# Dilated attention's second stage: places of GpSimd's transfers, a fourth maxima tile, gate and high part in two steps, later residual loads

## The chip, the cores and the metric

The program runs on one NeuronCore of a Trainium2 chip. The metric is device microseconds of one execution. An engine has its own instruction stream and works through it in order: TensorE (PE, its weight loads PEld), VectorE (DVE), ScalarE (ACT), GpSimd (POOL) and SyncE (SP). Semaphores tie them together. A transfer is issued from a queue of one of these engines and lands later; an instruction that waits holds up all that stands behind it on its engine.

## The reference

A trunk of two layers on a sequence of 1024 tokens with 1024 channels, all in float32: layer 0 mixes by a gated short convolution, layer 1 by dilated attention. Only the second part of layer 1 is touched. For 16 head slots and three dilation groups (windows and dilations 128/1, 512/4, 2048/16) it computes

```python
for g, (window, dilation) in enumerate(DILATED_GROUPS):
    q = rms_norm(qkv[:, :, g, 0], q_gain[g])
    k = rms_norm(qkv[:, :, g, 1], k_gain[g])
    o, l = dilated_group_attention(q, k, qkv[:, :, g, 2], bias_g, window, dilation)
...
alpha = jax.nn.softmax(jnp.stack(lses, axis=0), axis=0)
o = jnp.sum(alpha[..., None] * jnp.stack(outs, axis=0).astype(jnp.float32), axis=0)
y = o.reshape(B, S, ATTN_WIDTH).astype(h.dtype) * jax.nn.silu(z)
return y @ w_out        # and the layer adds x
```

where a group's attention is the softmax over a causal band of 128-query blocks with a table of position biases, and l is the log of its denominator.

## The kernel before

The convolution layer and the projection of the attention layer come first and leave q and k (qkd), v (vd), silu(z) (zd) and the residual stream (x1d) in device memory. The second stage takes them from there. Its work is cut into 24 units: eight pairs of heads (hp 0 to 7), each with groups g = 0, 1, 2. A unit has 4, 4 and 2 steps for the three groups, so a pair has ten and the stage has 80 steps; step 0 of pair hp is step 10 hp of the stage. Steps below are counted over the whole stage unless "of its pair" is said.

The order on each engine is written out by hand: a loop over k goes through the parts of the steps that are due, in the order of lags (0, 1, LC = 4, 3, 5 to 16, LB = 2), then the exps, then the dense tiles (`extra`), then what is started ahead (`begins`). A part with lag n of step j is issued in turn k = j + n. Within a turn, each engine gets its instructions in that order.

A step has four parts. A: scores on PE (L904, L918, L923) and on DVE, for each block and head, an addition of the bias that also takes the running minimum of the negated scores into the unit's small tile `nl` (L936). E: the exps on ACT (L942), which also leave the row sums in `nl`. B, two turns later: transposes on PE (L949) into a bank of `pt`, copied to `pts` by DVE (L860) or ACT (L862). C, four turns later: the product with V on PE (L963, L970) and, when a half of the output is complete, its copy into `o` by DVE (L982, L985).

The three groups of a pair are merged by their denominators. The groups order tokens differently, so the maxima and sums of groups 0 and 1 go through device memory on POOL's queue: `store` writes `nl` to `nld` (L994 for g = 0, L997 twice for g = 1), and for g = 2 loads them back in its own order into `ml` (L992, twice). `weights` takes the overall maximum on DVE (L1006 to L1009) and one exp on ACT (L1010). `shares` makes the three factors `fo` on DVE (L1019 to L1024), `store_shares` writes them to `fd` (L1028, twice), and `spread` reads each back over 64 partitions, into `fb` for w = 2 and 1 and into `sqacc` for w = 0 (L1033, six transfers). `scale` multiplies a group's output by its factor (L1036, three times on DVE), `add` sums two of them on POOL (L1039, twice), `gate` multiplies by silu(z) in `sz` (L1042, DVE), `high` rounds the result to the first of two parts `y2` (L1046, ACT), and `low` takes the remainder (L1049, DVE). Pair 6 has an earlier schedule than pairs 0 to 5, and pair 7 ends the stage by other means (`wide`, `spread_last`, `last`).

The tile `nl` has three buffers that the units take in turn; `begin` takes a new one in the first part A of a unit. `fo`, `ml`, `f`, `mx` and `sqacc` have one buffer each.

The output projection rides along: `some` computes one of 16 tiles of the output for two pairs at a time, six matmuls a step (L1133 to L1135), from step k0 = (first step of pair 2r + 2) + LD on; in the next turn DVE adds the sum to the tile's accumulator (`add_sums`, L1169), which `residual` filled from x1d (L1150) on SP's queue. The third block starts at step 74 and runs past the loop's 80 steps. `fetch`, `split` (L1144) and `split_low` (L1147) bring in the weights of the projection and cut them in two parts. SP's queue also carries the loads of q and k (`loads`), V (`load_v`), sz (`load_z`) and the bias tables (`prefetch`).

Of the kernel before, what the change touches and what calls it, by code (L numbers as in the profile page):

```python
# [10 lines left out]
F32 = mybir.dt.float32  # L11
F32R = mybir.dt.float32r
I32 = mybir.dt.int32
AF = mybir.ActivationFunctionType
# [21 lines left out]
def trunk(ctx: ExitStack, tc: tile.TileContext, a, out):  # L36
# [778 lines left out]
    with tc.tile_pool(name="sp", bufs=1, space=PSUM) as sp, tc.tile_pool(name="ptp", bufs=2, space=PSUM) as ptp, \  # L815
# [48 lines left out]
        def attention(hp, g):  # L864
# [18 lines left out]
            def begin():  # L883
                u["nl"] = sm.tile([P, 8, 4], F32, name="nl", tag="nl", bufs=3)

# [114 lines left out]
            def weights():  # L1000
# [8 lines left out]
                nc.vector.tensor_tensor(f[:, :, 2], mx[:, :, 0], nm, op=OP.subtract)  # L1009
                nc.scalar.activation(f, f, AF.Exp)  # L1010
                u["f"] = f, mx
# [23 lines left out]
            def scale(w):  # L1035
                nc.vector.tensor_tensor(O[hp, w], O[hp, w], u["fb", w], op=OP.mult)  # L1036
# [66 lines left out]
            end = steps[-1]  # L1103
            end.setdefault(0 if g == 2 else 1, []).append(store)
            if g == 2:
# [6 lines left out]
                else:  # L1112

                    e = -1 if hp == HP - 2 else 1 - hp % 2
                    w = 2 if e < 0 else 3
                    todo = [(w, weights), (w + 1, shares), (w + 1, store_shares), (w + 1, lambda: spread(2)),
                            (w + 1, lambda: spread(1)), (w + 1, lambda: spread(0)), (e + 9, lambda: scale(2)),
                            (e + 10, lambda: scale(1)), (e + 10, lambda: add(2)), (e + 11, lambda: scale(0)),
                            (e + 11, lambda: add(0)), (e + 13, gate), (e + 13, high), (e + 14, low)]
                for lag, f in todo:  # L1120
# [3 lines left out]
        LB, LC = 2, 4  # L1124
        LD = 14
        W, ending = {}, {}
# [30 lines left out]

        sums = []

# [28 lines left out]
        for i, (dt, hf) in enumerate(tiles):  # L1188
            when(3 + 2 * i, residual, dt, hf)
        for r in range(3):  # L1190
# [11 lines left out]
        for kt in range(KT):  # L1202
            k = at[kt // 2 * 2 + 2, 0][0] + 4 + kt % 2 if kt < 6 else len(steps) - 6 + kt % 2
            when(k - 5 - kt % 2, fetch, kt)
            when(k, split, kt)
            when(k + 2, split_low, kt)
# [5 lines left out]
        while k < len(steps) + LC - 1 or any(x >= k for x in extra):  # L1212
# [4 lines left out]
            for f in steps[k].get("exps", ()) if k < len(steps) else ():  # L1217
                f()
            for f in extra.get(k, ()):
                f()  # L1220
            for f in begins.get(k, ()):
                f()
            k += 1

# [93 lines left out]
```

## Time and profile before

| | |
|---|---|
| median of three runs | 1984.29 us (1981.63 to 1986.51) |
| the profiled execution | 1977.11 us |
| its span on the page | 1975.3 us |
| attention's second stage, loop | from about 1626 us on |
| transfers from 1625 to 1960 us | 66.69 MB, 199 GB/s on average |

The page divides the span into 40 slices, with a busy share in tenths for each engine and the TensorE clock that was granted:

```profile
PE   8999999999999999999999999999999998798998
...
DVE  7866765666576555788889689868998867788896
ACT  6433333333334453444343443334334338777670
POOL 0356657766665211334434344444434351332330
PEclk9999999999999999999999999999999998899999
DMA  6312232222224574413233233323233357976752
GB/s 197 116 57 92 82 107 76 95 93 78 96 65 158 181 237 166 141 67 119 95 117 118 79 114 107 122 72 128 88 106 107 106 174 252 268 222 200 211 146 86
```

A slice is 49.4 us wide; the second stage fills the last seven, from slice 33 on (counted from 0). A busy share there says how much of a slice an engine worked, not what it waited for: that is read from the waits view and the timeline, in which a row gives the start, the duration, the engine and line, output and inputs, and in brackets the idle time ahead of the instruction with the instruction or transfer that ended it.

### The profile page before, as it was taken

The numbers are of one execution on the slowest core, as the hardware profiler recorded it, in microseconds if no ns is written. First come the engines' busy times: TensorE is split into PE (matmuls) and PEld (weight loads), VectorE is DVE, ScalarE is ACT, GpSimd is POOL, SyncE is SP. The second block draws the span as 40 slices with busy tenths as digits, with TensorE's granted clock in tenths as the row PEclk, the third lists the DMA queues.
The fourth block names the chain that finished last, engine by engine and source line by source line (L and its number), as shares of the span: only waits on it lengthen the run. The fifth ranks groups of instructions, "written<-read, shape, count | busy, mean of one in ns | idle before, by whom it ended". The sixth has DMA issues, their size and how long they took to land.

```text
span 1975.3 us, 30620 instructions
## 1 busy us (share of the span) xinstructions
PE 1910.9 (97%) x10894; PEld 1553.3 (79%) x10894; DVE 1495.4 (76%) x2769; ACT 885.8 (45%) x2031; POOL 848.5 (43%) x767
## 2 busy tenths in 40 slices
PE   8999999999999999999999999999999998798998
PEld 6888888888888888878878888788888876576767
DVE  7866765666576555788889689868998867788896
ACT  6433333333334453444343443334334338777670
POOL 0356657766665211334434344444434351332330
PEclk9999999999999999999999999999999998899999
DMA  6312232222224574413233233323233357976752
GB/s 197 116 57 92 82 107 76 95 93 78 96 65 158 181 237 166 141 67 119 95 117 118 79 114 107 122 72 128 88 106 107 106 174 252 268 222 200 211 146 86
DMA packets 116777, 253.79 MB, mean 128 GB/s; under 512 B 17598, under 2 KB 22814, under 8 KB 116624
## 3 DMA queue, kind: packets, MB, share of 16 engines
q1 hardware_dynamic: 93280, 176.89, 28.0%
q0 software_dynamic: 23344, 74.95, 11.3%
q8 instruction: 85, 1.39, 0.3%
q14 instruction: 68, 0.56, 0.1%
HBM read 192.53 MB, written 67.64 MB: 132 GB/s over the span
## 4 chain that ended last, share of the span: by engine, by line
PE 77%; DVE 12%; issue 5%; DMA 3%; ACT 3%; POOL 1%; SPq 0%; DVEq 0%; POOLq 0%; ACTq 0%
PE pp L301 18%; PE pp L304 18%; PE pp L303 17%; PE pp L552 3%; PE pp L551 3%; PE pp L553 3%; DVE ws L165 2%; PE pt L949 2%; PE po L970 2%; DVE blkc L716 1%; PE pp L374 1%; PE pp L375 1%; PE pp L376 1%; DMA nld<-nl 1%; ACT xs L942 1%
## 5 line engine op out<-in xcount | busy, mean ns | idle before, releaser
L165 DVE TENSOR_TENSOR ws<-wr,ws 128x512 fp32r<-128x512 f32 x284 | 279.0, 984 | 120.9 <-ACT ws L164 119.5
L164 ACT ACTIVATE ws<-wr 128x512 fp32r<-128x512 f32 x284 | 178.3, 630 | 357.9 <-PE pp L304 232.6
L164 ACT ACTIVATE ws<-sr 128x512 fp32r<-128x512 f32 x272 | 169.9, 629 | 293.2 <-PE pp L304 235.7
L276 POOL TENSOR_TENSOR sr<-wr 128x512 f32<-128x512 f32 x136 | 186.6, 1372 | 259.9 <-DMA wr<-in_wqk 59.2
L165 DVE TENSOR_TENSOR ws<-sr,ws 128x512 fp32r<-128x512 f32 x272 | 226.6, 840 | 70.9 <-ACT ws L164 68.7
L313 DVE TENSOR_TENSOR f<-pp,f 128x512 f32<-128x512 f32 x204 | 139.6, 684 | 91.0 <-PE pp L304 84.3
L942 ACT ACTIVATE xs<-xs,nl 128x256 f32<-128x256 f32 (+2 forms) x384 | 160.5, 425 | 5.4 <-DVE nl L936 5.3
L309 ACT ACTIVATE f<-pp 128x512 f32<-128x512 f32 x228 | 132.5, 581 | 27.8 <-POOL blkc L682 12.5
L671 ACT ACTIVATE f<-f 128x512 f32<-128x512 f32 x96 | 60.7, 632 | 139.2 <-DVE f L313 101.8
L276 POOL TENSOR_TENSOR sr<-wr,sr 128x512 f32<-128x512 f32 x68 | 88.5, 1301 | 70.7 <-issue 47.8
L936 DVE CUSTOM_DVE_ANT_0 xs<-ps,bt 128x256 f32<-128x256 f32 (+2 forms) x384 | 102.3, 325 | 21.8 <-PE ps L923 8.8
L301 PE MATMUL pp<-blkg,ws 128*128 128x512 f32 x272 | 107.2, 394 | 3.5 <-ACT f L309 3.5
L301 PE MATMUL pp<-blkf,ws 128*128 128x512 f32 x272 | 108.5, 399 | 0.7 <-ACT f L309 0.7
L301 PE MATMUL pp<-blka,ws 128*128 128x512 f32 x272 | 107.1, 394 | 0.7 <-ACT f L309 0.7
L301 PE MATMUL pp<-blkb,ws 128*128 128x512 f32 x272 | 107.4, 395 | 0.0
L301 PE MATMUL pp<-blkd,ws 128*128 128x512 f32 x272 | 106.9, 393 | 0.0
L304 PE MATMUL pp<-blkf,ws 128*128 128x512 f32 x272 | 106.3, 391 | 0.0
L304 PE MATMUL pp<-blkb,ws 128*128 128x512 f32 x272 | 106.0, 390 | 0.0
L304 PE MATMUL pp<-blka,ws 128*128 128x512 f32 x272 | 106.0, 390 | 0.0
L304 PE MATMUL pp<-blkd,ws 128*128 128x512 f32 x272 | 106.0, 390 | 0.0
L303 PE MATMUL pp<-blkb,ws 128*128 128x512 f32 x272 | 105.9, 389 | 0.0
L303 PE MATMUL pp<-blka,ws 128*128 128x512 f32 x272 | 105.9, 389 | 0.0
(341 smaller groups left out, 5270.4 us busy)
## 6 DMA issues: line engine op xcount, KB each, us to landing
wr<-in_conv_w_in SPq DMA_DIRECT2D x128, 256.0 KB, 3.1
wr<-in_wqk SPq DMA_DIRECT2D x96, 256.0 KB, 3.0
qkd<-blkc POOLq DMA_DIRECT2D x48, 512.0 KB, 3.4
qk<-qkd SPq DMA_DIRECT2D x48, 512.0 KB, 5.2
wr<-in_conv_w_out SPq DMA_DIRECT2D x64, 256.0 KB, 3.2
f<-in_x SPq DMA_DIRECT2D x48, 256.0 KB, 4.3
wr<-in_wv SPq DMA_DIRECT2D x48, 256.0 KB, 3.1
vd<-f POOLq DMA_DIRECT2D x48, 256.0 KB, 2.6
```

Source lines behind the costliest of these rows:

```text
L164: nc.scalar.activation(t[:, 0], src, AF.Copy)
L165: nc.vector.tensor_tensor(t[:, 1], src, t[:, 0].bitcast(F32), op=OP.subtract)
L276: nc.gpsimd.tensor_tensor(t, x, y, op=op)
L301: nc.tensor.matmul(ps, w[:, 0, ws], b[:, k, 0], start=new and k == 0, stop=False, skip_group_check=not new)
L303: nc.tensor.matmul(ps, w[:, 0, ws], b[:, k, 1], start=False, stop=False, skip_group_check=not new)
L304: nc.tensor.matmul(ps, w[:, 1, ws], b[:, k, 0], start=False, stop=end and k == 3, skip_group_check=not new)
L309: nc.scalar.activation(t, ps, AF.Copy)
L313: nc.vector.tensor_tensor(m, ps, m, op=OP.add)
L551: nc.tensor.matmul(ps[dt], w[:, 0, ws], b[:, k, 0], start=(q == k == 0), stop=False)
L671: nc.scalar.activation(sq, t, AF.Square)
L936: nc.vector.tensor_tensor_reduce(out=x, in0=flat[s][:, cols], in1=u["bt"][s][:, bs], op0=OP.add, op1=OP.min, scale=-1.0, scalar=3e38, accu ...
L942: nc.scalar.activation(x, x, AF.Exp, bias=nm, scale=-1.0, accum_out=L)
```

## The change

Counted in the whole stage, for pair hp with first step 10 hp:

- `nl` has four buffers instead of three.
- The stores of groups 0 and 1 keep their lag of 1. The load of `ml` moves from lag 0 of the pair's last step to lag 2 for pairs 0 and 1 and lag 1 for pairs 2 to 5; pairs 6 and 7 keep 0.
- `weights` moves from step 12 to 13 for pairs 0 and 1 and stays at 12 for pairs 2 to 5. `shares` and `store_shares` move from 13 to 14, `spread` from 13 to 16. The three `scale` stay at 19, 20, 21 for even pairs and go from 18, 19, 20 to the same places for odd pairs, with `add` in the steps of the last two.
- `gate` goes from 23 to 22 for even pairs and stays at 22 for odd ones; `high` is at 23 and `low` at 24 for both (before: 23 and 24 for even, 22 and 23 for odd pairs). Pair 6 keeps its places (weights 11, shares 12, scales 17 to 19, gate and high 21, low 22) except for `spread`, which goes from 12 to 13.
- The exp of `weights` is put in a list, `behind`, that is emptied after the exps of the turn.
- LD is 15 instead of 14: the dense tiles are at steps 35 to 50, 55 to 70 and from 75 on instead of 34, 54 and 74; five instead of six tiles of the third block lie within the 80 steps.
- The 16 residual loads are at steps 31 to 46, one a step, instead of 3, 5, ... 33.
- The split of every odd row of the projection's weights, both its parts, comes a step later; the fetches stay.

```diff
@@ -881,7 +881,7 @@
                 u["bt"] = bt
 
             def begin():
-                u["nl"] = sm.tile([P, 8, 4], F32, name="nl", tag="nl", bufs=3)
+                u["nl"] = sm.tile([P, 8, 4], F32, name="nl", tag="nl", bufs=4)
 
             def nml(j, s):
                 return u["nl"][:, j, s:s + 1], u["nl"][:, j, 2 + s:3 + s]
@@ -1007,7 +1007,7 @@
                 nc.vector.tensor_tensor(mx[:, :, 0], mx[:, :, 0], nm, op=OP.min)
                 nc.vector.tensor_tensor(f[:, :, 0:2], mx.to_broadcast([P, 8, 2, 2]), ml[:, :, :, 0:2], op=OP.subtract)
                 nc.vector.tensor_tensor(f[:, :, 2], mx[:, :, 0], nm, op=OP.subtract)
-                nc.scalar.activation(f, f, AF.Exp)
+                behind.append(lambda: nc.scalar.activation(f, f, AF.Exp))
                 u["f"] = f, mx
 
             def shares():
@@ -1101,7 +1101,7 @@
                     st = make(js, not steps)
                     steps.append({lag: [f] for lag, f in zip((0, LB, LC, "exps"), st)})
             end = steps[-1]
-            end.setdefault(0 if g == 2 else 1, []).append(store)
+            end.setdefault(1 if g < 2 else 2 if hp < 2 else 1 if hp < HP - 2 else 0, []).append(store)
             if g == 2:
                 if hp == HP - 1:
                     steps[-2][3] = steps[-2].pop(LC)
@@ -1111,18 +1111,20 @@
                     ending.update(turn=end.pop(LB)[0], weights=weights, spread=spread_last, last=last)
                 else:
 
-                    e = -1 if hp == HP - 2 else 1 - hp % 2
-                    w = 2 if e < 0 else 3
-                    todo = [(w, weights), (w + 1, shares), (w + 1, store_shares), (w + 1, lambda: spread(2)),
-                            (w + 1, lambda: spread(1)), (w + 1, lambda: spread(0)), (e + 9, lambda: scale(2)),
-                            (e + 10, lambda: scale(1)), (e + 10, lambda: add(2)), (e + 11, lambda: scale(0)),
-                            (e + 11, lambda: add(0)), (e + 13, gate), (e + 13, high), (e + 14, low)]
+                    todo = [(2, weights), (3, shares), (3, store_shares), (4, lambda: spread(2)),
+                            (4, lambda: spread(1)), (4, lambda: spread(0)), (8, lambda: scale(2)),
+                            (9, lambda: scale(1)), (9, lambda: add(2)), (10, lambda: scale(0)),
+                            (10, lambda: add(0)), (12, gate), (12, high), (13, low)] if hp == HP - 2 else [
+                            (4 if hp < 2 else 3, weights), (5, shares), (5, store_shares), (7, lambda: spread(2)),
+                            (7, lambda: spread(1)), (7, lambda: spread(0)), (10, lambda: scale(2)),
+                            (11, lambda: scale(1)), (11, lambda: add(2)), (12, lambda: scale(0)),
+                            (12, lambda: add(0)), (13, gate), (14, high), (15, low)]
                 for lag, f in todo:
                     end.setdefault(lag, []).append(f)
             return steps, prefetch
 
         LB, LC = 2, 4
-        LD = 14
+        LD = 15
         W, ending = {}, {}
 
         def dense(ps, kts, dt, hf, first, last):
@@ -1155,7 +1157,7 @@
             t = scores() if name == "ps" else ptp.tile([P, 4, P], F32, name=name, tag=name)
             return t.rearrange("p a b -> p (a b)")
 
-        sums = []
+        sums, behind = [], []
 
         def some(kts, dt, hf, name):
 
@@ -1186,7 +1188,7 @@
             if un[1] == 2:
                 when(k - 1, load_z, un[0])
         for i, (dt, hf) in enumerate(tiles):
-            when(3 + 2 * i, residual, dt, hf)
+            when(31 + i, residual, dt, hf)
         for r in range(3):
             k0 = at[2 * r + 2, 0][0] + LD
             k = k0
@@ -1200,8 +1202,8 @@
                                                some((2 * r, 2 * r + 1), dt, hf, name))
                 k += (i % 2 if i < 13 else 0) if late else 1
         for kt in range(KT):
-            k = at[kt // 2 * 2 + 2, 0][0] + 4 + kt % 2 if kt < 6 else len(steps) - 6 + kt % 2
-            when(k - 5 - kt % 2, fetch, kt)
+            k = (at[kt // 2 * 2 + 2, 0][0] + 4 if kt < 6 else len(steps) - 6) + 2 * (kt % 2)
+            when(k - 5 - 2 * (kt % 2), fetch, kt)
             when(k, split, kt)
             when(k + 2, split_low, kt)
         when(len(steps), ending["turn"])
@@ -1216,10 +1218,14 @@
                     f()
             for f in steps[k].get("exps", ()) if k < len(steps) else ():
                 f()
+            while behind:
+                behind.pop()()
             for f in extra.get(k, ()):
                 f()
             for f in begins.get(k, ()):
                 f()
+            while behind:
+                behind.pop()()
             k += 1
```

How the instructions stand on the engines, at three places. First POOL's queue, from the load of pair 0's maxima on, before (DMA rows are transfers; `x2` is two of a kind in a row):

```order
L992 DMA ml<-nld 64x64 x2
L1028 DMA fd<-fo 64x6x8 x2
L1033 DMA fb<-fd 64x1024 x4
L1033 DMA sqacc<-fd 64x1024 x2
L994 DMA nld<-nl 128x8x4
L997 DMA nld<-nl 512x1x4 x2
L992 DMA ml<-nld 64x64 x2
L1039 TENSOR_TENSOR o<-o 128x1024 x2
```

and in the changed kernel:

```order
L992 DMA ml<-nld 64x64 x2
L994 DMA nld<-nl 128x8x4
L1028 DMA fd<-fo 64x6x8 x2
L1033 DMA fb<-fd 64x1024 x4
L1033 DMA sqacc<-fd 64x1024 x2
L997 DMA nld<-nl 512x1x4 x2
L1039 TENSOR_TENSOR o<-o 128x1024 x2
L992 DMA ml<-nld 64x64 x2
```

Pair 1's store of group 0 (L994) now stands ahead of pair 0's factors and their spread, and pair 1's load of `ml` behind pair 0's two additions.

Second, DVE in steps 42 to 44, as the difference of the two orders, where pair 2 is gated (L1042) and pair 3 weighted (L1006 to L1009, then L1019 to L1024). Step 42:

```order
 L1008 TENSOR_TENSOR f<-mx,ml 128x8x4
 L1009 TENSOR_TENSOR f<-mx,nl 128x8x2
+L1042 TENSOR_TENSOR sz<-o,sz 128x1024
 L860 COPY pts<-pt 128x384
-L1169 TENSOR_TENSOR acc<-pd,acc 128x512
+L1171 TENSOR_TENSOR acc<-pd,acc 128x512
```

The gate is now behind pair 3's weights (the addition of a dense tile only has another line number). The piece with the shares, step 43 before and 44 in the changed kernel:

```order
 L1023 RECIPROCAL mx<-mx 128x16
 L1024 TENSOR_TENSOR fo<-f,mx 128x8x6
-L1042 TENSOR_TENSOR sz<-o,sz 128x1024
```

The gate no longer stands behind the shares.

Third, ACT in steps 41 to 43 before, with the exp of pair 3's weights (L1010) and pair 2's high part (L1046):

```order
L862 ACTIVATE pts<-pt 128x256 x2
L942 ACTIVATE xs,nl<-xs,nl 128x256 x4
L1010 ACTIVATE f<-f 128x48
L862 ACTIVATE pts<-pt 128x384
L942 ACTIVATE xs,nl<-xs,nl 128x256 x4
L1046 ACTIVATE y_15555<-sz 128x1024
L862 ACTIVATE pts<-pt 128x512 x2
```

and in the changed kernel:

```order
L862 ACTIVATE pts<-pt 128x256 x2
L942 ACTIVATE xs,nl<-xs,nl 128x256 x4
L862 ACTIVATE pts<-pt 128x384
L942 ACTIVATE xs,nl<-xs,nl 128x256 x4
L1010 ACTIVATE f<-f 128x48
L1046 ACTIVATE y_15525<-sz 128x1024
L862 ACTIVATE pts<-pt 128x512 x2
```

The exp of the weights now follows the exps of its step instead of standing ahead of that step's copy; the high part stays ahead of the copies of the next step.

## The prediction

> **What bounds the kernel now.** First the head of the page and its clock row, then the windows view by head pair, since a share of the whole span hides the one stage that is edited.
>
> ```profile
> span 1975.3 us, 30620 instructions
> ...
> PEclk9999999999999999999999999999999998899999
> ```
>
> The profiled execution took 1977.11 us, 1.8 us more than its span and 7.2 us under the median 1984.29. The sum is made against 1977.1, and its difference is then taken from the median. The granted clock falls under 0.9 in only two of the 40 slices, from 1630 to 1728 us, inside the edited stage. Everything before 1626 us is the same code in both kernels.
>
> ```profile
> 1626.00:1649.00 23.00, 20.75 (x301) 15.20 (x301) 18.15 (x103) 20.77 (x80) 3.48 (x4) 1.00 0.83 270
> 1649.00:1683.00 34.00, 27.18 (x413) 21.48 (x410) 23.94 (x127) 25.02 (x111) 8.70 (x14) 0.85 0.76 238
> 1683.00:1724.00 41.00, 28.89 (x407) 21.66 (x406) 30.97 (x121) 27.88 (x113) 12.71 (x15) 0.83 0.96 263
> ```
>
> Columns: stretch, length, busy PE, PEld, DVE, ACT, POOL with counts, granted clock, DMA share, GB/s. The rows are ten steps each: pairs 0, 1 and 2. Pair 0 takes 2.3 us a step at full clock; pairs 1 and 2 take 34 and 41 us though no engine is busy for more than 31. The rest is waiting. PE's timeline gives the places; the bracket is the idle time ahead of the row and its releaser.
>
> ```profile
> 1664.73 1.94 PE L949 MATMUL pt<-ident,xs 128*128 128x128 f32 x8 [6.54 <-DVE pts L860]
> ...
> 1693.27 1.55 PE L923 MATMUL ps<-qk 64*64 64x192 f32 x14 [7.12 <-DVE nl L936]
> ...
> 1702.29 1.06 PE L949 MATMUL pt<-ident,xs 128*128 128x128 f32 x8 [1.01 <-DVE pts L860]
> ...
> 1704.51 0.88 PE L970 MATMUL po<-pts,V 128*64 128x128 f32 x12 [0.51 <-DVE o L982]
> ...
> 1708.19 2.00 PE L949 MATMUL pt<-ident,xs 128*128 128x128 f32 x8 [2.80 <-DVE pts L860]
> ...
> 1737.29 0.63 PE L949 MATMUL pt<-ident,xs 128*128 128x128 f32 x4 [3.53 <-DVE pts L860]
> ...
> 1782.45 1.20 PE L949 MATMUL pt<-ident,xs 128*128 128x128 f32 x8 [2.87 <-ACT pts L862]
> ...
> 1810.82 0.44 PE L949 MATMUL pt<-ident,xs 128*128 128x128 f32 x2 [0.61 <-DVE pts L860]
> ...
> 1816.47 0.63 PE L949 MATMUL pt<-ident,xs 128*128 128x128 f32 x4 [0.91 <-DVE pts L860]
> ...
> 1860.58 1.14 PE L949 MATMUL pt<-ident,xs 128*128 128x128 f32 x8 [2.86 <-ACT pts L862]
> ...
> 1889.68 0.44 PE L949 MATMUL pt<-ident,xs 128*128 128x128 f32 x2 [1.36 <-DVE pts L860]
> ...
> 1896.52 0.63 PE L949 MATMUL pt<-ident,xs 128*128 128x128 f32 x4 [2.10 <-DVE pts L860]
> ```
>
> After a gap PE runs at a lower clock, which the windows behind the gaps show:
>
> ```profile
> 1665.00:1686.00 21.00, 21.00 (x270) 16.34 (x268) 17.68 (x89) 18.22 (x80) 6.89 (x11) 0.86 0.82 231
> 1693.00:1705.00 12.00, 10.21 (x160) 7.99 (x162) 11.77 (x42) 6.70 (x27) 5.81 (x4) 0.79 0.91 302
> 1708.00:1734.00 26.00, 24.32 (x378) 18.47 (x378) 21.99 (x103) 25.40 (x104) 10.36 (x14) 0.93 0.94 274
> 1738.00:1779.00 41.00, 40.80 (x484) 31.63 (x486) 34.34 (x140) 29.04 (x121) 12.69 (x15) 0.96 0.76 219
> 1783.00:1815.00 32.00, 30.98 (x387) 23.17 (x390) 26.80 (x105) 25.43 (x103) 11.30 (x13) 0.95 0.60 180
> 1861.00:1888.00 27.00, 27.00 (x308) 20.22 (x306) 21.95 (x82) 22.14 (x92) 8.75 (x12) 0.94 0.76 234
> ```
>
> A gap's price is its idle time plus (1 − clock) × window. A, step 12: 6.54 + 0.14 × 21 = 9.5 us. B, step 20: 7.12 + 0.21 × 12 = 9.6. C, steps 22 to 24: 1.01 + 0.51 + 2.80 + 0.07 × 26 = 6.1. D, step 32: 3.53 + 0.04 × 41 = 5.2. E, step 43: 2.87 + 0.05 × 32 = 4.5. F, steps 50 to 53: 1.5. G, step 63: 2.86 + 0.06 × 27 = 4.5. H, steps 70 to 73: 3.5. Together 44.4 us, the most there is to gain.
>
> The Trainium skill, "TensorE: Matmul & The Clock Gate", § "HAM oscillation — how this bites in real kernels", asks for no idle gap of PE above about 3.4 us. The row at 1782.45 disagrees: half clock follows a gap of 2.87 us. By that rule the short left-over gaps below would carry no half clock, and the sum would be −24 instead of −21.
>
> Who holds PE at A and B stands on DVE, at E and G on ACT:
>
> ```profile
> 1663.42 0.18 DVE L1006 TENSOR_TENSOR mx<-ml 128x16 f32<-128x16 f32 x1 [6.53 <-DMA ml<-nld]
> ...
> 1692.57 0.29 DVE L936 CUSTOM_DVE_ANT_0 xs<-ps,bt 128x128 f32<-128x128 f32 x1 [7.38 <-DMA nld<-nl]
> ...
> 1779.60 1.22 DVE L1042 TENSOR_TENSOR sz<-o,sz 128x1024 f32<-128x1024 f32 x1
> ```
> ```profile
> 1780.85 1.06 ACT L1046 ACTIVATE y<-sz 128x1024 fp32r<-128x1024 f32 x1 [3.81 <-DVE sz L1042]
> ```
> ```profile
> DVE mx L1006 <- DMA ml<-nld: 8.9, 2, 6.5
> ACT y L1046 <- DVE sz L1042: 16.3, 7, 3.8
> ```
>
> At A, DVE's weights wait 6.53 us for the ml load, and the copies that PE needs stand behind them. At B the next unit's minima need a free nl tile, whose store is late. At E and G ACT's high waits for the gate, with ACT's copies behind it.
>
> **The change, part by part.** *Fourth nl tile and POOL's order (B).* POOL's rows say why that store was late:
>
> ```profile
> 1676.37 2.10 POOL L1033 DMA_DIRECT2D fb<-fd  x4 [5.91 <-PE pt L949]
> ...
> 1693.73 1.08 POOL L992 DMA_DIRECT2D ml<-nld  x2 [11.70 <-DMA nld<-nl]
> ...
> 1885.80 2.39 POOL L1039 TENSOR_TENSOR o<-o 128x1024 f32<-128x1024 f32 x1
> ```
>
> The spread held the queue for 5.91 + 2.10 us, pair 1's stores left behind it, and the last took 11.7 us to land. Now unit (2,0) takes the tile of (0,2), last read by pair 0's shares in step 14, and (1,0)'s store is ahead of fd. B goes in full.
>
> *Later weights (A and C).*
>
> ```profile
> 1665.88 1.89 DVE L982 COPY o<-po 128x512 f32<-128x512 f32 x2
> ...
> ml<-nld POOLq DMA_DIRECT2D x16, 16.0 KB, 5.3
> ```
>
> Weights of pair 0 move from step 12 to 13. One more step of DVE's work now stands ahead of them: four L936 (0.29 in the row at 1692.57, more for wider ones) and L982, 4 × 0.29 + 1.89 = 3.1, with a copy of pt some 3.7 us. The ml load is asked for a step later too, but its store lands no earlier than before, so nothing is charged for that. Of the 6.53 us 2.8 stay, with half of A's clock loss 4.2 us (A'). For pair 1 the load now stands behind pair 0's two adds: the second waits for scale(0) of step 21 and takes 2.39 us, the load lands 5.3 us later, and the weights come two steps of 2.5 us after step 21. That leaves a wait of 1.5 to 3 us; with its clock 3.3 (C').
>
> For A, B and C together I take the floor by the busiest engine: ACT 25.0 us in pair 1, DVE 31.0 in pair 2, 56.0, plus A' 4.2 and C' 3.3 = 63.5 us instead of 34 + 41 = 75: **−11.5**. Best end: A, B and C gone and both waits hidden, −19 (75 − 56); worst: only B gone and A' and C' as long as A and C are, −9.6, or 0 if a later load takes its place.
>
> *Pair 2 (D).* Its weights and gate keep their place; the second wait of L1006 (8.9 − 6.5 = 2.4 us) stays. Expected 0, from −5.2 to +3 (a load that lands 3 us later).
>
> *Gate a step ahead of high, exp behind the step's exps (E, G).* DVE used to do shares, gate (1.22 us) and the finishing copies within a step; now the gate is a step earlier, and high follows it by a step instead of waiting 3.81 us. ACT's exp of the weights no longer stands ahead of copies. DVE is nearly as busy as PE there (34.34 of 41), so some 1 us stays: **−3.5 each, −7.0**; bounds 0 and −9.0.
>
> *Scales of odd pairs a step later (F, H).*
>
> ```profile
> 1882.51 1.22 DVE L1036 TENSOR_TENSOR o<-o,fb 128x1024 f32<-128x1024 f32 x1
> ...
> 1885.76 3.52 DVE L1036 TENSOR_TENSOR o<-o,sqacc 128x1024 f32<-128x1024 f32 x1
> ```
>
> The same product takes 1.22 or 3.52 us; the long one lies beside POOL's add, in the row at 1885.80 above. If the new places keep them apart, that is 2.3 us back at H. I take F −1, H −2: **−3.0**, bounds 0 and −5.
>
> *Residual loads, dense blocks one step later.* Loads of 256 KB go from steps 3 to 33 to steps 31 to 46. Their first use is step 36 for tile 0, five steps behind the load:
>
> ```profile
> acc<-x1d SPq DMA_DIRECT2D x16, 256.0 KB, 6.6
> ...
> nld<-nl POOLq DMA_DIRECT2D x16, 8.0 KB, 6.4
> ```
>
> 6.6 us against five steps: hidden; if the cover were gone, one add would wait a few us. A step with a dense tile takes 3.84 us (from 1737.29 to 1782.45 in eleven steps, less the gap), one without 2.3; the one tile more behind the loop costs between 0 and that 1.5: **+0.5**.
>
> **Sum:** −11.5 + 0 − 7.0 − 3.0 + 0.5 = −21.0: 1956.1 against the profiled 1977.1, **1963.3 against the median**. The terms' bounds add up to −38 and +4.5.
>
> **The rivals.** *Short landings.* If stores and loads land near their shortest, A' and C' vanish: −21 − 4.2 − 3.3 = −28.5, **1955.8**. The 8 KB row above has a median of 6.4 us, against it; that it is measured among loads of share 0.8 to 0.96, which the residual loads leave, is for it. The Trainium skill, "DMA: Bandwidth & Descriptors", § "Anatomy of one DMA — SWDGE (gpsimd) path", gives such a transfer about 2 us plus its bytes over the rate; the row's 6.4 us is three times that, so the trace disagrees.
>
> *Spread late.* Pair 0's fd leaves in step 14, its spread moves from step 13 to 16, and scale(2) stays at 19.
>
> ```profile
> fb<-fd POOLq DMA_DIRECT2D x28, 256.0 KB, 4.9
> ...
> DMA to landing us min/median/max: 2.7/5.6/11.8
> ```
>
> From fd's issue: up to 7.3 us till fb leaves (landing 5.6 plus issue), then 4.9 to 11.8 us, so 12.2 to 19 us, against five steps of 2.5 = 12.5. If the long end holds in pairs 0 and 1, scale(2) waits some 5 us in each: +10, sum −11, **1973**.
>
> *The waits only move.* Pair 1's ml load behind the adds, and landings of 11.7 us as in the row above: weights of pairs 0 and 1 wait as long as now, B's gain goes into qk or V loads at share 0.96, only about 4 us of E and G are left: 1984.3 − 4, **1980**, not to be told from no change.
>
> *Slower: residual loads collide.* In 1738 to 1779 the DMA share is 0.76 already. A load of 0.262 MB in each step, at the 302 GB/s of the row from 1693, is 0.87 us of 3.84, so 0.23 more: 0.99. Say that landings on POOL's queue then take 2.1 times as long (11.8 over 5.6). The weights of pair 3 at step 42 follow a store and a load, 6.4 + 5.3 = 11.7 us, now 12.9 longer; those of pair 2 at step 32 lose on the load alone, 5.8; pair 2's way from fd to scale(2), 12.2 us as above, becomes 25.6 against five steps of 3.84 = 19.2, 6.4 late; three clock drops like D's cost 4.8. Together 29.9, so −21 + 30 = +9, **1993**. It overtakes the gain from landings about 1.8 times as long.
>
> **How the numbers follow.** Forecast 0.48, short landings 0.17, spread late 0.17, waits only move 0.10, collision 0.08. A difference under 0.3% (6 us) can't be told from no change. Faster by more: 0.48 + 0.17 + 0.17, less 0.03 for their upper ends above 1978 = 0.79; same 0.10 + 0.03 = 0.13; slower 0.08. The range runs from 1946, where every term meets its best bound (1984.3 − 38), to 1981, just past the third rival; it leaves out the collision and what of that rival lies above, 0.2 at most.
>
> **What would show it.** Right: no L936 row waiting for nld<-nl; L1006 waiting under 3 us in steps 13 and 23; L1046 waiting near 0; clock near 1.0 from 1683 on; the two pairs done in about 63 us. Wrong: waits of L1036 for fb<-fd or sqacc<-fd in steps 19 to 21 (spread late), waits of L1006 above 3 us, an add of L1171 waiting for acc<-x1d, or a DMA share near 1.0 in steps 31 to 46 with late ml loads (collision). The forecast is wrong as a whole if PE still shows gaps of 3 us or more in pairs 1 and 2.

## The result, and the profile after

The changed kernel takes 1972.52 us (median of five runs, 1965.93 to 1975.44) against 1984.08 us before (1981.54 to 1986.51): ratio 0.9937 with a 95% interval of 0.9914 to 0.9959, 11.6 us or 0.6% faster. The forecast was 1963.3 in a range from 1946 to 1981: right in direction, 21.0 us where 11.6 came, nearly twice too large in size. The profiled execution took 1968.56 us, so against the profile of before the difference is 8.55 us. Of that, 1.2 us go the other way ahead of the edited stage, whose first scores start at 1627.16 instead of 1625.94 us; the stage itself is 9.8 us shorter.

Where it went is read from the windows view, cut at each pair's first scores on PE. Before, pairs 1 to 6, pair 7 with the loop's end, and the tail; the columns are stretch, length, busy time of PE, PEld, DVE, ACT and POOL with counts, granted clock, DMA share and GB/s:

```profile
1649.39:1682.99 33.60, 26.78 (x407) 21.24 (x406) 23.54 (x123) 24.62 (x109) 8.70 (x14) 0.85 0.76 237
1682.99:1724.14 41.15, 29.04 (x408) 21.67 (x407) 31.12 (x123) 28.03 (x114) 12.71 (x15) 0.83 0.96 263
1724.14:1763.18 39.04, 34.66 (x443) 26.63 (x442) 30.87 (x136) 30.47 (x128) 12.67 (x15) 0.96 0.83 242
1763.18:1805.42 42.24, 39.37 (x467) 30.11 (x467) 36.51 (x136) 29.83 (x117) 12.68 (x15) 0.96 0.66 210
1805.42:1841.32 35.90, 33.42 (x443) 24.95 (x442) 30.47 (x128) 27.93 (x115) 12.69 (x15) 1.00 0.69 198
1841.32:1883.52 42.20, 39.34 (x467) 30.01 (x466) 36.51 (x136) 29.72 (x117) 12.67 (x15) 0.96 0.76 233
1883.52:1938.00 54.48, 49.45 (x630) 38.26 (x630) 50.22 (x161) 34.96 (x134) 18.46 (x19) 1.00 0.33 88
1938.00:1975.00 37.00, 31.45 (x171) 25.34 (x169) 21.87 (x35) 1.27 (x2) 0.00 (x0) 0.99 0.31 114
```

After, the same for pairs 1 to 7 and the tail:

```profile
1650.61:1676.47 25.86, 24.26 (x408) 18.89 (x407) 22.79 (x121) 24.40 (x109) 8.75 (x14) 1.00 0.79 248
1676.47:1712.86 36.39, 28.51 (x408) 21.06 (x407) 29.88 (x126) 27.65 (x109) 12.62 (x15) 0.91 0.85 244
1712.86:1754.20 41.34, 34.13 (x438) 25.87 (x437) 31.43 (x134) 31.53 (x133) 12.70 (x15) 0.92 0.91 261
1754.20:1792.22 38.02, 38.00 (x468) 29.11 (x467) 35.31 (x135) 29.84 (x117) 12.76 (x15) 1.00 0.96 291
1792.22:1831.04 38.82, 35.85 (x444) 27.68 (x443) 31.36 (x129) 27.95 (x115) 12.75 (x15) 0.91 0.76 226
1831.04:1869.06 38.02, 37.99 (x468) 29.11 (x467) 35.62 (x135) 29.73 (x117) 12.72 (x15) 1.00 0.69 207
1869.06:1927.00 57.94, 52.09 (x631) 40.47 (x630) 54.04 (x163) 36.00 (x135) 18.42 (x19) 0.94 0.36 102
1927.00:1966.50 39.50, 33.89 (x175) 27.48 (x174) 21.69 (x35) 0.63 (x1) 0.00 (x0) 0.96 0.29 107
```

Pair 0 has 23.45 us in both. Pairs 4 and 6 now run at PE's pace (38.00 busy of 38.02) at full clock; pair 5 and the end have *lost* clock (pair 5 from 1.00 to 0.91, the two rows of the end from 1.00 and 0.99 to 0.94 and 0.96). From the last pair's first scores to the last matmul it is 87.6 us before and 93.5 after. The gaps of 1.5 us and more that are left on PE's timeline:

```profile
1681.28 0.44 PE L949 MATMUL pt<-ident,xs 128*128 128x128 f32 x2 [2.43 <-DVE pts L860]
...
1699.13 0.66 PE L949 MATMUL pt<-ident,xs 128*128 128x128 f32 x4 [1.60 <-DVE pts L860]
...
1729.62 1.12 PE L949 MATMUL pt<-ident,xs 128*128 128x128 f32 x4 [5.53 <-DVE pts L860]
...
1805.09 0.66 PE L949 MATMUL pt<-ident,xs 128*128 128x128 f32 x4 [2.06 <-DVE pts L860]
...
1880.59 0.71 PE L923 MATMUL ps<-qk 64*64 64x192 f32 x11 [2.50 <-DVE nl L936]
...
1908.38 0.50 PE L1135 MATMUL pd<-y,y 128*128 128x512 f32 x1 [1.55 <-DVE acc L1171]
```

and what DVE waits for around the first three, on its own timeline:

```profile
1679.39 1.23 DVE L1036 TENSOR_TENSOR o<-o,fb 128x1024 f32<-128x1024 f32 x1 [2.11 <-DMA fb<-fd]
...
1683.64 1.23 DVE L1036 TENSOR_TENSOR o<-o,fb 128x1024 f32<-128x1024 f32 x1 [1.31 <-DMA fb<-fd]
...
1688.24 1.23 DVE L1036 TENSOR_TENSOR o<-o,sqacc 128x1024 f32<-128x1024 f32 x1 [1.07 <-DMA sqacc<-fd]
...
1697.78 0.17 DVE L1006 TENSOR_TENSOR mx<-ml 128x16 f32<-128x16 f32 x1 [0.89 <-DMA ml<-nld]
...
1726.66 0.79 DVE L1006 TENSOR_TENSOR mx<-ml 128x16 f32<-128x16 f32 x1 [4.63 <-DMA ml<-nld]
```

The waits of before for nld at step 20 and for ml at step 12 are gone. In their place DVE waits for the spread in steps 19 to 21, 0.89 us for pair 1's ml at step 23, and at step 32 for pair 2's ml 4.63 us instead of 2.34: 10.0 us in these five rows, where the three waits of before were 6.53, 7.38 and 2.34, some 16 us.

### The profile page after: what moved, and what is told of

It reads as the page before. It is cut to its first block, busy times and chain, and to the rows that moved or that the text cites. A ratio compares the mean times of both kernels' runs of the same rounds, so it can differ in the third digit from the quotient of the medians.

```text
span 1966.8 us, 30588 instructions
## 1 busy us (share of the span) xinstructions
PE 1913.9 (97%) x10894; PEld 1555.4 (79%) x10894; DVE 1495.3 (76%) x2769; ACT 886.9 (45%) x2031; POOL 847.6 (43%) x767
## 5 line engine op out<-in xcount | busy, mean ns | idle before, releaser
L165 DVE TENSOR_TENSOR ws<-wr,ws 128x512 fp32r<-128x512 f32 x284 | 274.4, 968 | 120.8 <-ACT ws L164 119.3
L936 DVE CUSTOM_DVE_ANT_0 xs<-ps,bt 128x256 f32<-128x256 f32 (+2 forms) x384 | 102.5, 325 | 12.5 <-PE ps L923 7.4
L301 PE MATMUL pp<-blka,ws 128*128 128x512 f32 x272 | 107.3, 394 | 0.7 <-ACT f L309 0.7
L301 PE MATMUL pp<-blkd,ws 128*128 128x512 f32 x272 | 106.9, 393 | 0.0
L276 POOL TENSOR_TENSOR sr<-sr,wr 128x512 f32<-128x512 f32 x68 | 104.0, 1529 | 4.9
L304 PE MATMUL pp<-blka,ws 128*128 128x512 f32 x272 | 106.0, 390 | 0.0
```

The costliest lines, as they stand in the source:

```text
L165: nc.vector.tensor_tensor(t[:, 1], src, t[:, 0].bitcast(F32), op=OP.subtract)
L276: nc.gpsimd.tensor_tensor(t, x, y, op=op)
L301: nc.tensor.matmul(ps, w[:, 0, ws], b[:, k, 0], start=new and k == 0, stop=False, skip_group_check=not new)
L304: nc.tensor.matmul(ps, w[:, 1, ws], b[:, k, 0], start=False, stop=end and k == 3, skip_group_check=not new)
L936: nc.vector.tensor_tensor_reduce(out=x, in0=flat[s][:, cols], in1=u["bt"][s][:, bs], op0=OP.add, op1=OP.min, scale=-1.0, scalar=3e38, accu ...
```

## The experiments

All are compared with the kernel before on the same chip. The table has each run's ratio with its interval and, from its profile, two lengths of the stage: pairs 1 to 3, where DVE waits for transfers, and from pair 4's first scores to the last matmul. The dense tile that moved from step 34 to the end takes 1.4 us out of the first and into the second wherever LD is 15. Each length is from one profile. The first varies by several us between kernels that differ in nothing there; the second repeats within about 1 us. Of an edit only the places that change are shown; the rest of the line is left out.

| kernel | ratio (95%) | pairs 1 to 3 | pair 4 to the end |
|---|---|---|---|
| before | | 113.8 | 208.0 |
| changed | 0.9937 (0.9914 to 0.9959) | 103.6 | 208.4 |
| before_nl4 | 0.9993 (0.9981 to 1.0005) | 115.6 | 206.9 |
| spread14 | 0.9932 (0.9916 to 0.9949) | 106.8 | 208.4 |
| resid_old | 0.9953 (0.9937 to 0.9970) | 110.2 | 207.9 |
| gate_old | 0.9993 (0.9981 to 1.0004) | 109.9 | 213.1 |
| ld14 | 0.9948 (0.9931 to 0.9965) | 109.1 | 207.8 |
| nl3 | 0.9946 (0.9928 to 0.9964) | 103.3 | 208.8 |
| w33 | 0.9943 (0.9928 to 0.9959) | 108.7 | 208.7 |
| exp_old | 0.9943 (0.9925 to 0.9961) | 108.7 | 208.0 |
| scale35 | 0.9916 (0.9895 to 0.9937) | 109.9 | 205.0 |
| half_k | 0.9903 (0.9887 to 0.9920) | 98.9 | 207.7 |
| scale35_split | 0.9908 (0.9889 to 0.9926) | 106.9 | 203.7 |
| late01 | 0.9873 (0.9859 to 0.9886) | 103.2 | 200.7 |

One landing goes with most of the scatter of the first length: that of the last part of the spread, sqacc, by its median between 1650 and 1760 us. Among the kernels with the change it takes 6.9 to 9.2 us (8.7 in the changed kernel) where pairs 1 to 3 take 98.9 to 103.6, and 11.2 to 12.5 us (12.5 in scale35) where they take 106.8 to 109.9; resid_old, with 7.3 at 110.2, is the exception. What makes it land early or late isn't known.

**The fourth buffer alone**, in the kernel before:

```diff
-u["nl"] = sm.tile([P, 8, 4], F32, name="nl", tag="nl", bufs=3)
+u["nl"] = sm.tile([P, 8, 4], F32, name="nl", tag="nl", bufs=4)
```

> The kernel before with the fourth nl buffer alone. If the stall at step 20 (7.1 us of PE, 9.6 with its clock) was a matter of the buffer, it goes: no L936 row waits for nld<-nl, pair 2 (41.2 us) comes to 31 to 34, and the time falls by 8 to 10 us, close to the whole change. If the store behind the spread would be missed next by something else (pair 1's ml load still leaves behind it, and C and D stay), pair 2 stays above 36 us and the time falls by under 6.

1983.50 us, no change that can be told. PE's timeline of this kernel:

```profile
1703.63 1.94 PE L949 MATMUL pt<-ident,xs 128*128 128x128 f32 x8 [7.97 <-DVE pts L860]
```

and DVE's:

```profile
1702.32 0.18 DVE L1006 TENSOR_TENSOR mx<-ml 128x16 f32<-128x16 f32 x1 [7.37 <-DMA ml<-nld]
```

The 7.12 us gap at step 20 is gone, and 7.97 us stand at step 22, where the weights wait for the load that left behind the same spread. One cause had two places to wait, and the later one takes what the earlier gives up.

**Three buffers** in the changed kernel:

```diff
-u["nl"] = sm.tile([P, 8, 4], F32, name="nl", tag="nl", bufs=4)
+u["nl"] = sm.tile([P, 8, 4], F32, name="nl", tag="nl", bufs=3)
```

> The changed kernel with three nl buffers. The fourth buffer alone gave the kernel before nothing. If the order on POOL's queue does B's work (the store of the pair's first group leaves ahead of the factors), no L936 row waits for nld<-nl and the time stays within 2 us of the changed kernel. If both are needed, a wait of 3 to 7 us stands at step 20 or 24 again and the time rises by 4 to 9 us.

1973.05 us, and no L936 row waits for nld<-nl. The new places do B's work without the buffer, which does nothing measurable in either kernel. That it is the order on POOL's queue is read from POOL's rows: pair 1's first store leaves ahead of the factors, at 1664.25 in the changed kernel. No run puts that order back by itself.

**The gate back**:

```diff
-(12, lambda: add(0)), (13, gate), (14, high), (15, low)]
+(12, lambda: add(0)), (14 - hp % 2, gate), (14 - hp % 2, high), (15 - hp % 2, low)]
```

> The changed kernel with gate, high and low where they were (even pairs 23, 23, 24; odd pairs 22, 22, 23). If the gate ahead of the high part is what freed steps 43 and 63, PE waits there some 2.9 us again, pairs 4 and 6 go from 38.0 to about 42 each, the time rises by 7 to 8 us. If the exp behind the step's exps did it, pairs 4 and 6 stay at 38 to 39. Where no dense tile covers DVE (step 52), the gate leaves the weights' step: pair 5 falls from 38.8 to about 36.

1983.04 us: nearly all of the gain is lost with these three places. PE's timeline shows steps 43 and 63 stalling again, and the waits view why:

```profile
1782.59 1.15 PE L949 MATMUL pt<-ident,xs 128*128 128x128 f32 x8 [2.56 <-ACT pts L862]
...
1860.08 1.97 PE L949 MATMUL pt<-ident,xs 128*128 128x128 f32 x8 [1.81 <-ACT pts L862]
```
```profile
ACT y L1046 <- DVE sz L1042: 29.9, 6, 8.5
```

In the changed kernel the same view has 4.9 us in 4 waits, the longest 2.1. Of the 29.9 us only 5.06 and 4.05 belong to steps 43 and 63; the longest wait stands at step 32:

```profile
1737.38 1.06 ACT L1046 ACTIVATE y<-sz 128x1024 fp32r<-128x1024 f32 x1 [8.51 <-DVE sz L1042]
```

Pairs 4 and 6 take 40.8 and 41.2 us instead of 38.0, pair 5 37.9, 1.0 less; from pair 4 to the end it is 4.7 us more. The rest of the 10 us lies in pairs 1 to 3 (109.9), at the upper end of what other variants show there. Part of it comes from the same places: at steps 23 and 32 PE stands 4.03 and 8.02 us, where DVE's wait for ml is 1.51 and 6.27; in the changed kernel it is 1.60 and 5.53 with 0.89 and 4.63. The remainder is not separated from the scatter.

**The exp at once**:

```diff
-behind.append(lambda: nc.scalar.activation(f, f, AF.Exp))
+nc.scalar.activation(f, f, AF.Exp)
```

> The changed kernel with the exp of the weights issued at once on ACT, ahead of the step's copies and exps. If the gate alone freed steps 43 and 63, pairs 4 and 6 stay at 38.0 and the loss is confined to step 32, where the exp waits for late weights with the copies behind it: up to 3 us. If the exp mattered in each pair, pairs 4 and 6 come to 40 or more and the time rises by 4 to 8 us.

1973.66 us, as the changed kernel. Pair 6 stays at 38.0; pair 4 comes to 42.3 in the profile, where ml happened to be 3.19 us late at step 42 and ACT's copies stood behind the exp. PE's gap of 2.29 us ended there with ACT's copy, and 0.29 us more with DVE's, which the late weights hold up too; so that the later exp insures against late loads is likely, not shown. It has a price: with the exp at once pair 5 takes 36.5 us instead of 38.8, and pair 7 with the end 91.2 instead of 93.5, though the scales are at their new places. These two lengths stay at 38.2 and above and, the moved tile counted in, at 92.8 and above in the other kernels that keep the scales, gate and exp of the change.

**The residual loads back**:

```diff
-when(31 + i, residual, dt, hf)
+when(3 + 2 * i, residual, dt, hf)
```

> The changed kernel with the residual loads at steps 3, 5, ... 33 as before. If they made room for the small transfers, the landings in pairs 1 and 2 grow: weights at step 13 wait again (up to 6.5 us), pair 1 goes from 25.9 to above 28, the time up by 3 to 8 us. If they only moved traffic, pairs 1 and 2 keep their lengths and pair 3, from which they are taken, loses part of the 4.6 us wait at step 32: time equal or 1 to 4 us less.

1975.53 us; the intervals overlap, so a gain of about 3 us from the later loads is possible, not shown. Pair 1 goes to 31.1 us, with the weights waiting 2.39 us at step 13, as the first theory has it; but nl3, which has the late loads, comes to 29.3 with a wait of 1.99. In no profile with the late loads does an L1171 row wait for acc<-x1d, nor does the share of 0.96 in pair 4 stop PE: the collision did not come.

**The spread two steps earlier**, in the step of the factors:

```diff
-(7, lambda: spread(2)), (7, lambda: spread(1)), (7, lambda: spread(0)),
+(5, lambda: spread(2)), (5, lambda: spread(1)), (5, lambda: spread(0)),
```

> The changed kernel with pairs 0 to 5 spreading right behind their factors (step 14 of a pair, before the change 13, changed 16). Theory 'spread late': the scales at steps 19 to 21 no longer wait 2.1 + 1.3 + 1.1 us for fb and sqacc, the nld stores of step 18 no longer fall among the spread's 1.5 MB, so pair 2's weights at step 32 wait under 2 us instead of 4.6; pairs 2 and 3 together come from 77.7 to 70 or less, the time falls by 5 to 8 us. Rival: the waits come from elsewhere (DVE, the load of ml behind the adds), and pairs 2 and 3 stay above 75; or the first store waits behind fd again and L936 stalls at step 20.

1972.80 us, no gain. DVE waits 13.3 us for ml, fb and sqacc in steps 13 to 32 instead of 10.0. The edit hardly moves the transfer: the spread leaves 4.9 and 6.1 us behind fd's issue in pairs 0 and 1, against 5.6 and 5.2 in the changed kernel, and in pair 1 the profile names fd's landing as what it waits for. So this run doesn't tell what an earlier spread would be worth.

**Pair 2's weights at step 33**:

```diff
-(4 if hp < 2 else 3, weights)
+(4 if hp < 3 else 3, weights)
```

> The changed kernel with pair 2's weights a step later (step 33 instead of 32), as pairs 0 and 1 have it. If the wait of 4.6 us at step 32 is the chain store, landing, load, landing against four steps without a dense tile, a step more of 2.4 us and its DVE work takes most of it: the wait falls to 0 to 2 us and pair 3 from 41.3 to 36 to 38, time down by 3 to 6 us. If the wait moves to the factors or the spread (steps 34 to 39), the time stays.

1973.04 us, no gain. The wait of DVE for ml is gone altogether, and it waits at other places instead:

```profile
1720.37 1.23 DVE L1036 TENSOR_TENSOR o<-o,fb 128x1024 f32<-128x1024 f32 x1 [3.17 <-DMA fb<-fd]
...
1726.12 1.22 DVE L1036 TENSOR_TENSOR o<-o,sqacc 128x1024 f32<-128x1024 f32 x1 [2.22 <-DMA sqacc<-fd]
...
1733.56 1.23 DVE L1042 TENSOR_TENSOR sz<-o,sz 128x1024 f32<-128x1024 f32 x1 [4.84 <-POOL o L1039]
```

The longest of these is the gate's, at step 32. It waits for POOL's adds, and these stand on POOL's queue behind pair 2's load of ml, which waits for its store to land:

```profile
1727.65 1.08 POOL L992 DMA_DIRECT2D ml<-nld  x2 [13.77 <-DMA nld<-nl]
```

The same late landing reaches DVE by another way, and PE stands 3.97 us for it at step 32.

**The dense blocks back**:

```diff
-LD = 15
+LD = 14
```

> The changed kernel with the dense blocks at steps 34, 54 and 74 as before. Pairs 5 and 7 came out 2.9 and 5.9 us longer (1.4 of the 5.9 is the dense tile that now falls into step 70). If the dense tile in steps 50 and 70 and its absence in 54 and 74 is the cause (PE is not covered while DVE has weights, gate and factors), pair 5 returns to 36 and pair 7 with the tail to 88 to 89, time down by 4 to 8 us. If it is the gate in the weights' step, pair 5 stays at 38 to 39; if it is a product slowed beside POOL's add (L1008 took 2.2 us instead of 0.19 at step 72), pair 7 keeps its 2.5 us gap.

1974.21 us. Pair 5 stays at 39.6 and pair 7 with the end at 92.2, which is the one tile. My first theory for the lost clock fell with it.

**Scales of pairs 3 and 5 back**:

```diff
+o = int(hp in (3, 5))
-(10, lambda: scale(2)), (11, lambda: scale(1)), (11, lambda: add(2)), (12, lambda: scale(0)), (12, lambda: add(0)),
+(10 - o, lambda: scale(2)), (11 - o, lambda: scale(1)), (11 - o, lambda: add(2)), (12 - o, lambda: scale(0)), (12 - o, lambda: add(0)),
```

> The changed kernel with the three scales and two adds of pairs 3 and 5 a step earlier, where they were before (steps 48, 49, 50 and 68, 69, 70). If the later places are what lengthened pairs 5 and 7 (the last scale now stands in the step ahead of the next pair's weights, the add of POOL beside them: L1006 1.25 us, L1008 2.22 instead of 0.19), pair 5 goes from 38.8 to about 36, pair 7 with the tail from 93.5 to 89 to 91, time down by 4 to 7 us, to 1966 to 1969. If the tail has another cause, pair 7 stays at 93 and the gain is at most 3.

1966.81 us, the six executions from 1964.10 to 1975.16 and the profiled one at 1974.34. The interval overlaps the changed kernel's, so the reading rests on the lengths: pair 5 comes to 36.3, as expected; pair 7 only to 92.3, so the end had another cause too. What the later scales do at step 72 stands in the changed kernel's timelines, POOL's and DVE's:

```profile
1877.36 2.36 POOL L1039 TENSOR_TENSOR o<-o 128x1024 f32<-128x1024 f32 x1 [2.39 <-DVE mx L1006]
...
1904.27 2.37 POOL L1039 TENSOR_TENSOR o<-o 128x1024 f32<-128x1024 f32 x1 [1.25 <-DVE o L1036]
```
```profile
1877.54 2.22 DVE L1008 TENSOR_TENSOR f<-mx,ml 128x32 f32<-128x32 f32 x1
...
1904.71 3.02 DVE L1149 TENSOR_TENSOR y<-wraw,y 128x1024 fp32r<-128x1024 f32 x1
```

L1008, 0.19 us elsewhere, starts 0.18 us into POOL's add and ends with it (1879.76 and 1879.72). At step 52 it is L1006, 0.16 us in scale35, that lies beside the add from 1800.51 to 1802.88: it starts at 1801.66 and takes 1.25 us.

In the changed kernel scale(0), weights and gate stand in two steps without a dense tile, and PE gets its copies late. The second pair of rows is the other cause, and the next run's question.

**In addition the odd splits back**:

```diff
-k = (at[kt // 2 * 2 + 2, 0][0] + 4 if kt < 6 else len(steps) - 6) + 2 * (kt % 2)
-when(k - 5 - 2 * (kt % 2), fetch, kt)
+k = (at[kt // 2 * 2 + 2, 0][0] + 4 if kt < 6 else len(steps) - 6) + kt % 2
+when(k - 5 - kt % 2, fetch, kt)
```

> The last one with the scales of pairs 3 and 5 a step earlier, and in addition the split of the projection's odd weight rows where it was (a step earlier). In the changed kernel the second part of row 7 (L1149) starts beside an add of POOL and takes 3.02 us instead of 1.22, and PE waits 1.55 us for the sum behind it. If that is it, L1149 takes 1.22 again, the 1.55 us gap goes, pair 7 with the tail comes from 92.3 to 89 to 91, time 1 to 3 us less than without it: 1964 to 1966. If an add meets it all the same, pair 7 stays.

DVE's row for the same product (one line further down) in this kernel:

```profile
1904.05 1.22 DVE L1150 TENSOR_TENSOR y<-wraw,y 128x1024 fp32r<-128x1024 f32 x1
```

It takes 1.22 us again, the 1.55 us gap is gone, and pair 7 with the end takes 91.1. The time is 1969.09 us, with a ratio 0.0008 lower than scale35 and overlapping intervals: the mechanism is shown in the rows, its 1.1 us not in the time.

**Half of q and k**, for pairs 1 to 3. This kernel leaves out half of these loads, so what it computes is not the layer; it serves for the time alone:

```diff
-QK[hp, g] = [ap.tile([P, S], F32, name="qk", tag="qk", bufs=6) for _ in range(2)]
-for i in range(2):
+few = hp in (1, 2, 3)
+QK[hp, g] = [ap.tile([P, S], F32, name="qk", tag="qk", bufs=6) for _ in range(1 if few else 2)]
+if few:
+    QK[hp, g] *= 2
+for i in range(1 if few else 2):
```

> The changed kernel in which pairs 1 to 3 load one of the two 512 KB tiles q and k of a unit and use it for both (the scores of these pairs are of q with itself): 1.5 MB less of some 9 MB per pair, all on SP's queue, and no other instruction moved. If the waits of DVE for fb, sqacc and ml in steps 19 to 21, 29 to 32 come from transfers that share the DMA engines with bulk loads, they fall to under a third of the 7 to 10 us that the changed kernel and its variants show, pairs 2 and 3 from 77.7 to 69 or less, time down by 5 to 9 us. If they come from places on POOL's queue alone, they stay above 6 us and the time within 2 us.

1965.19 us, and all four runs lie between 1963.55 and 1966.33. Pairs 1 to 3 take 98.9 us, the least of all. DVE's waits for the spread and ml (the lines stand three further down in this kernel, so L1039 is the scale and L1009 the weights):

```profile
1687.43 1.22 DVE L1039 TENSOR_TENSOR o<-o,sqacc 128x1024 f32<-128x1024 f32 x1 [2.08 <-DMA sqacc<-fd]
...
1723.90 1.56 DVE L1009 TENSOR_TENSOR mx<-ml 128x16 f32<-128x16 f32 x1 [2.79 <-DMA ml<-nld]
```

That is 4.9 us and 0.6 in two more rows, about half of the changed kernel's 10.0 but not under a third as expected, and nl3 had 6.1 by scatter alone. Pairs 2 and 3 take 73 us, not 69 or less, and the interval overlaps the changed kernel's. That the bulk loads take part in the lateness is likely, not shown.

**A step more for pairs 0 and 1** and pair 2's weights at step 33, on top of scale35_split:

```diff
-o = int(hp in (3, 5))
+o = -1 if hp < 2 else int(hp in (3, 5))
-(4 if hp < 2 else 3, weights)
+(4 if hp < 3 else 3, weights)
-(12 - o, lambda: add(0)), (13, gate), (14, high), (15, low)]
+(12 - o, lambda: add(0)), (13 + int(hp < 2), gate), (14 + int(hp < 2), high), (15 + int(hp < 2), low)]
```

> In addition, pairs 0 and 1 have scales, gate, high and low a step later (six steps after the factors instead of five), and pair 2 its weights at step 33. If DVE's waits for fb and ml in steps 19 to 33 are a matter of slack, a step of 2.4 us more takes over half of them (16 us in the profile with the scales alone moved, 10 in that of the changed kernel): under 6 us in all, pairs 2 and 3 together from 84 to under 77, time down by 4 to 8 us more. If the transfers set the pace there whatever waits for them, the waits move to other transfers (ml, qk, V, bt) and pairs 1 to 3 keep 104 to 110 us: time within 3 us of the kernel without it.

1961.18 us, ratio 0.9873: the best of all, with an interval clear of the changed kernel's and, narrowly, of the one that it is built on. DVE's waits in pairs 1 to 3 for which the profile names a transfer are three:

```profile
1665.25 0.17 DVE L1006 TENSOR_TENSOR mx<-ml 128x16 f32<-128x16 f32 x1 [0.80 <-DMA ml<-nld]
...
1685.84 1.23 DVE L1036 TENSOR_TENSOR o<-o,fb 128x1024 f32<-128x1024 f32 x1 [0.67 <-DMA fb<-fd]
...
1700.84 0.17 DVE L1006 TENSOR_TENSOR mx<-ml 128x16 f32<-128x16 f32 x1 [3.89 <-DMA ml<-nld]
```

5.4 us in place of 13.8 in the kernel that it is built on. Two more rows belong to them, DVE's ahead of pair 0's scale(0) and POOL's of pair 1's load of ml:

```profile
1692.05 1.23 DVE L1036 TENSOR_TENSOR o<-o,sqacc 128x1024 f32<-128x1024 f32 x1 [3.28 <-issue]
...
1693.34 1.09 POOL L992 DMA_DIRECT2D ml<-nld  x2 [3.82 <-DMA nld<-nl]
```

For the 3.28 us the profile names no cause; sqacc, which this scale reads, is the likely one, and with it the waits are 8.6 us. The load of ml leaves ahead of pair 0's second add (1694.42) and waits for its store, so what is left at step 23 is that store's landing and not the adds. Pair 3 takes 36.5 us, where the kernels with the late residual loads otherwise have 40 to 47; pair 2 takes 40.2 instead of 36.2, at a clock of 0.79. Of the 6.8 us by which the stage is shorter, 3.8 lie in pairs 1 to 3 and 3.0 behind them. The gain in time is shown; that it is all slack isn't, since sqacc's median landing is also shorter in this profile, 8.9 us against 11.8.

## Why the prediction was right in direction and too large

By its own terms, with the lengths of the two profiles (the move of the dense tile taken out of pair 3 and of the end):

| term | forecast | measured |
|---|---|---|
| A, B, C (pairs 1 and 2) | −11.5 | −7.7 − 4.8 = −12.5 |
| D (pair 3) | 0 | +2.3 + 1.4 = +3.7 |
| E, G (pairs 4 and 6) | −7.0 | −4.2 − 4.2 = −8.4 |
| F, H (pairs 5 and 7) | −3.0 | +2.9 + 5.9 − 1.4 = +7.4 |
| dense tile | +0.5 | 0 |
| sum | −21.0 | −9.8 |

**The signs.** Those for the forecast came in part: no L936 row waits for nld<-nl, the weights at steps 13 and 23 wait 0 and 0.89 us, the two pairs take 62.3 us, and PE's longest gap in them is 2.43. Those against it came too: the scales of steps 19 to 21 wait for fb and sqacc, L1006 waits 4.63 us at step 32, and the clock is 0.91 and 0.92 in pairs 2 and 3.

**A, B, C: the sum right, its parts not.** The sum holds beyond this profile: nl3, exp_old, scale35 and scale35_split, which differ in little or nothing there, have 62.8 to 64.5 us for the two pairs. No run puts the later weights or POOL's order back alone, so A, B and C are not separated. A' was charged 4.2 us; pair 0's weights do not wait at all in this profile (up to 2.4 us in variants). C' was charged 3.3 us for a wait of up to 3; it is 0.89. In their place came the rival "spread late", which I had put at 0.17: three scales wait 4.5 us for fb and sqacc, and the clock in pair 2 comes to 0.91 (0.83 before), not near 1.0. It is no case of its own; some of it shows in nearly every variant. The forecast had it as an alternative where it belonged in the sum. That its 1973 is the time measured is chance: it cost 4.5 us and not 10, and other terms made up the rest.

**D: the step that failed in sign.** I kept pair 2's weights wait because its place doesn't move. But the spread now leaves two steps later, just ahead of the store whose landing the ml load follows: POOL waits 8.8 us for it instead of 6.0, and the wait of 2.3 us became 4.6. POOL's rows of this load, before and after:

```profile
1729.09 1.08 POOL L992 DMA_DIRECT2D ml<-nld  x2 [5.96 <-DMA nld<-nl]
...
1721.54 1.08 POOL L992 DMA_DIRECT2D ml<-nld  x2 [8.79 <-DMA nld<-nl]
```

Counted from pair 3's first scores, pair 1's spread starts 6.3 us ahead of them instead of nearly 11. That this is what delays the store is argued, not shown, since spread14 left the spread where it was; the residual loads are not it, for with them back the same weights wait 4.77 us. The miss of 3.7 us is near the low end: pair 3 takes 40.4 to 46.0 us in the four kernels just named, against 39.0 and 40.7 in the two profiles with the old places, each with the dense tile still in it.

**E, G: right, in mechanism and size.** The gate ahead of the high part does most of it: with these places back 2.7 and 3.2 of the 8.4 us are lost again. Where the other 2.5 us come from is not separated. The exp adds nothing to pair 6, where ml is in time.

**F, H: the failure that matters, 10.4 us.** The step was "if the new places keep them apart". They do, and no L1036 row of the changed kernel lies beside an add. But I looked at the product beside POOL's add and not at what the product was moved next to: the weights of the next pair, in steps with no dense tile for PE. Two short gaps and a lost clock came out, and scale35 takes back 2.5 us in pair 5 and 1.3 at the end. The scales are not the only way to it: exp_old leaves them where they are and has 2.3 us less in each, at a clock of 0.95 and 0.98 instead of 0.91 and 0.95, though PE's longest gap at the end is no shorter (2.89 us). So the 10.4 us are explained in part only. Likewise the odd splits, which I had not priced, moved L1149 onto an add.

**The rivals.** "The waits only move" is what the fourth buffer alone does, and in part what w33 does. The slower rival did not happen: no wait for residual loads, and pair 4 ran at PE's pace at a DMA share of 0.96. Short landings did not come either: the tile view of fd gives a median of 5.2 us (5.6 before) and a longest of 14.0.

## What to carry to other kernels

A wait that is removed pays only if what stands next on the same chain is not late too: look for every consumer of the late transfer before pricing the first. When an operation is moved, price its new neighbours on both engines, above all where the steps have no spare work to cover them. Where small transfers run beside bulk loads, plan their consumers by the long landings, not the median: the run that gave them a step more was the fastest here, while asking for the spread earlier hardly moved it and gained nothing.

## What the runs showed of the hardware

A product of DVE with both operands in SBUF that meets an add of POOL doesn't slow down in proportion: it ends with the add, or about its own length behind it. L1149 ends at 1907.73, POOL's add at 1906.64, and the product alone takes 1.22 us. Sums that read PSUM are not held: in the changed kernel this one lies within the add from 1872.61 to 1874.97.

```profile
1873.08 0.69 DVE L1171 TENSOR_TENSOR acc<-po,acc 128x512 f32<-128x512 f32 x1 [0.23 <-PE po L1137]
```

The Trainium skill, "SBUF — State Buffer", § "SBUF: two separate sides", states this as an exclusive lock on a port pair that DVE and GpSimd share, held for a whole instruction, against DVE operations with two inputs in SBUF; these rows agree.

The clock can fall after short gaps: in pair 5 of the changed kernel two, of 2.06 and 0.91 us, stand ahead of a stretch at half clock (the last three numbers are clock, DMA share and GB/s).

```profile
1809.00:1811.00 2.00, 2.00 (x10) 1.67 (x12) 1.90 (x7) 0.06 (x1) 1.43 (x2) 0.50 1.00 336
```

A gap of 2.10 us at step 73 before is followed by 1.00 from 1898.5 to 1902: the length of a gap alone doesn't decide it here. That is also why the end of the stage moved by more than its gaps: its clock is 0.95 from pair 7's first scores on, where before it was 1.00.
